# Masked decays of a gated DeltaNet mixer: products moved from GpSimd to ScalarE, masks into a TensorE pass, more buffers for the q, k, v sums

## Chip, cores and metric

The kernel runs on one core of a Trainium2 chip. The metric is the device time of one execution, in microseconds (us). Before the change it was 1235.73 us, the median of three runs (1235.57 to 1237.52).

## What is computed

A two-layer encoder on 256 tokens of width 1024. Each layer is half a feed-forward block, a mixer, and half a feed-forward block again. The change touches the mixer alone. One projection of the normed input, `h @ w_in`, gives the q, k, v of a gated DeltaNet (4 heads of 128), its output gate z, its decay logits, the two latents of an attention branch (8 heads) and two merge gates. The parts of the reference that the change bears on:

```python
def centred_short_conv(x, w):      # 5 taps over the sequence, then SiLU
    y = lax.conv_general_dilated(x, w[:, None, :], (1,), [(2, 2)], ...)
    return jax.nn.silu(y)
...
g = -exp(A_log) * softplus(a + dt_bias)                    # log decay per token and head, <= 0
gc = cumsum(to_chunks(g), axis=-1)
incl = jnp.tril(jnp.ones((C, C), bool))
decay = exp(where(incl, gc[..., :, None] - gc[..., None, :], -inf))
lower = where(strict, einsum("bhik,bhjk->bhij", kb, kc) * decay, 0.0)
unit = eye(C) + lower
uw = triangular_solve(unit, rhs, lower=True, unit_diagonal=True)
```

The recurrence runs in both directions over the sequence, each with its own decays, and the results are summed, normed, gated and projected; the attention branch is added, and the sum is projected back to the residual.

## The kernel before

Tokens lie in two tiles of 128. Every large product takes three passes on TensorE: a value is split in a rounded part and a rest (`whi` and `wlo` for weights, `xh` and `xl` or a pair `fr` for activations), and the passes are whi by xh, wlo by xh, whi by xl (L148 to L150, L557). For each tile of weights a DMA brings `raw`, ScalarE rounds it (L130, `whi`) and VectorE subtracts (L131, `wlo`). A `wlo` or a `whi` that comes late stops TensorE, and both engines take their instructions in a fixed order.

The order of the mixer's first half, as the code calls it: `rstd_row`, `qkv_group(2)`, the projection for beta, decay logits and the q latent, `qkv_group(3)`, `qkv_group(0)`, the projection for the kv latent, `gdn_scalars`, `gdn_decay(0)`, `lengths(4)`, `latent(cq)`, `qkv_group(1)`, `gdn_decay(1)`, `latent(ckv)`, `gdn_coeffs`, `gdn_la(1)`, `gdn_la(0)`, `mla_dense(0)`, `mla_heads`, `gdn_base`, then the projection for z. A scheduler merges these calls into one fixed order for each engine, by priority; `tc.high_priority(offset=n)` moves what stands under it forward by n places, as far as its inputs allow.

`qkv_group(grp)` makes two blocks of 128 channels of q (groups 0, 1), k (2, 3) or v (4, 5). Its 48 matmuls sum in a PSUM tile `acc`; VectorE scales the sum by the row `rb` into `pre` (L565), which is 4 columns wider than the sequence, with zeros at the rim (L563, L564, on GpSimd); ten VectorE instructions per group (L571 twice, L573 eight times) make the five taps into `cv`; ScalarE takes the tanh (L577, `th`) and VectorE finishes (L578) into `qkT`. `pre`, `cv` and `th` have one buffer each, and `lengths` uses the one of `cv` as well, for the squares of q or k (L586, on GpSimd). So the scaling of a group waits until the taps of the group before it are done, and its PSUM tile stays taken until then.

`gdn_decay(t)` makes, for token tile t and both directions d, the 128 by 128 decays of 4 heads at once. The log decays are split in `gh` and `gl`. For each of the two GpSimd multiplies an inclusive triangular mask (`m_le` or `m_ge`) by the log decay of each token, all heads in one instruction of 512 columns (L743, tile `pr`, three buffers); TensorE multiplies by the strict mask of the other side (L744), which sums the log decays between two tokens; ScalarE takes the exponential (L746, `g`); GpSimd multiplies by the inclusive mask again, to clear what lies on the wrong side (L755). `gdn_la` multiplies k by q and k (L763) and VectorE joins that with the decays (L767, `LA`). `gdn_base` starts the inversion of the triangular matrices: transposes on VectorE (L791, L796), 30 short GpSimd instructions in a chain (L805, L807), then blocks on TensorE (L839 and on).

Of the kernel before, what the change touches and what calls it, by code (L numbers as in the profile page):

```python
# [11 lines left out]
F32 = mybir.dt.float32  # L12
# [25 lines left out]
def encoder_trunk(ctx: ExitStack, tc: tile.TileContext, x, positions, norm_ffn1, ffn1_w_gate, ffn1_w_up,  # L38
# [286 lines left out]
    def mixer_consts(tmp):  # L325
# [30 lines left out]
        m_le = tri(const.tile([P, P], F32, name="m_le"), ALU.is_ge, -1, 1)  # L356
        m_ge = tri(const.tile([P, P], F32, name="m_ge"), ALU.is_ge, 1, -1)
        mr_gt, mr_lt = (const.tile([P, P], F32R, name=n) for n in ("mr_gt", "mr_lt"))
        V.tensor_copy(out=mr_gt, in_=tri(tp[:, 192:192 + P], ALU.is_gt, 1, -1))
        V.tensor_copy(out=mr_lt, in_=tri(tp[:, 320:320 + P], ALU.is_gt, -1, 1))  # L360
# [47 lines left out]
        for mul in (2.0 ** 11, 1.0):  # L408
# [4 lines left out]
            for c in split_const(per, 4):  # L413
# [7 lines left out]
        mc.update(alog=alog, dtb=dtb, ones=ones, m_le=m_le, m_ge=m_ge, mr_gt=mr_gt, mr_lt=mr_lt, half=half, mlo=mlo, mup=mup,  # L421
                  eye16=eye16, cos_t=cos_t, sin_t=sin_t)


    def mixer(l, next_gain):
# [4 lines left out]
        alog, dtb, ones, m_le, m_ge, mr_gt, mr_lt, half, mlo, mup, eye16, cos_t, sin_t = (  # L430
            mc[n] for n in ("alog", "dtb", "ones", "m_le", "m_ge", "mr_gt", "mr_lt", "half", "mlo", "mup", "eye16", "cos_t",
                            "sin_t"))
        with tc.tile_pool(name="mix", bufs=1) as mp:
            def t2(tag, bufs, shape=(P, NH, P)):
# [85 lines left out]
            def gdn_scalars():  # L520
                A.activation(out=beta, in_=ba[:, :, 0:8], func=AF.Exp, scale=-1.0)
                V.tensor_scalar(out=beta, in0=beta, scalar1=1.0, scalar2=None, op0=ALU.add)
                V.reciprocal(out=beta, in_=beta)
                V.tensor_tensor(out=sa, in0=ba[:, :, 8:16], in1=dtb[:, l:l + 1, :].to_broadcast([P, NT, 8]), op=ALU.add)

                V.scalar_tensor_tensor(out=se, in0=sa, scalar=-1.0, in1=sa, op0=ALU.mult, op1=ALU.min)
                A.activation(out=se, in_=se, func=AF.Exp)
                V.tensor_scalar(out=su, in0=se, scalar1=1.0, scalar2=None, op0=ALU.add)
                V.tensor_scalar(out=sc_, in0=su, scalar1=-1.0, scalar2=None, op0=ALU.add)
                V.tensor_tensor(out=sc_, in0=se, in1=sc_, op=ALU.subtract)  # L530
                A.activation(out=glog, in_=su, func=AF.Ln)
# [14 lines left out]
            def qkv_group(grp):  # L546
# [34 lines left out]
            def lengths(c0):  # L581

                pss = gdp()[:, :4 * NT * 32].rearrange("p (c t s) -> p c t s", c=4, t=NT)
                for c in (0, 2):
                    sq = t2("cv", 1, (P, 2, S))
# [143 lines left out]
                    V.tensor_tensor(out=nV[t], in0=ev4(pv), in1=bc(nk_[:, t, :]), op=ALU.mult)  # L729

            Es = {}
            gsp = [mp.tile([P, NT, 8], F32R, name=n) for n in ("gh", "gl")]

            def gdn_decay(t):

                for d in range(2):
                    lo_m, hi_m = (mr_gt, m_le) if d == 0 else (mr_lt, m_ge)
                    g4 = glog[:, t, d * 4:d * 4 + 4]
                    hb = hi_m[:, None, :].to_broadcast([P, NH, P])
                    pe = gdp()  # L740
                    for i in range(2):
                        gm = t2("pr", 3).bitcast(F32R)
                        G.tensor_tensor(out=gm, in0=hb, in1=bc(gsp[i][:, t, d * 4:d * 4 + 4].bitcast(F32)), op=ALU.mult)  # L743
                        T.matmul(pe, lhsT=lo_m, rhs=gm.rearrange("p h d -> p (h d)"), start=(i == 0), stop=(i == 1))  # L744
                    E = g2()
                    A.activation(out=E, in_=ev4(pe), func=AF.Exp)  # L746
                    if t == d:

                        V.tensor_copy(out=cs[d], in_=E[:, :, P - 1 if d == 0 else 0])
                    else:  # L750
                        pg = gdp()
                        T.matmul(pg[:, :NH], lhsT=hi_m, rhs=g4, start=True, stop=True)
# [366 lines left out]
```

## Time and profile before

| what | value |
|---|---|
| three runs, us | 1235.57, 1237.52, 1235.73 |
| profiled execution, us | 1238.92 |
| its span, us | 1237.2 |
| mean granted TensorE clock | 0.985 of full |
| TensorE busy | 1204.2 us, 97% |
| VectorE busy | 770.9 us, 62% |
| ScalarE busy | 622.4 us, 50% |
| GpSimd busy | 132.3 us, 11% |
| mixer of layer 0 | about 190 to 422 us |
| mixer of layer 1 | about 798 to 1042 us |

Times inside the trace are microseconds from the start of the span; a column that gives the mean of one instruction is in nanoseconds. The granted clock is a share of TensorE's full speed. The profiled execution is 3.2 us above the median, and its span leaves 1.7 us outside.

### The profile page before, as it was taken

How to read it: one execution, taken by the hardware profiler on the slowest of the kernel's cores; microseconds unless marked ns; L12 is line 12 of the kernel's file. 1: busy time of each engine (PE TensorE's matmuls, PEld its weight loads, DVE VectorE, ACT ScalarE, POOL GpSimd, SP SyncE). 2: the span in 40 equal slices, each digit the busy share in tenths (PEclk: the TensorE clock that was granted, in tenths of full speed). 3: DMA queues.
4: the chain of work that ended last, by engine and by line, in shares of the span. 5: the costliest groups of instructions: out<-in, count | busy, mean ns of one | idle time of the engine just before them, and what ended most of it. 6: DMA issues, size and time to landing. Idle time of an engine off the chain costs nothing.

```text
span 1237.2 us, 17605 instructions
## 1 busy us (share of the span) xinstructions
PE 1204.2 (97%) x7064; PEld 1016.9 (82%) x7064; DVE 770.9 (62%) x1125; ACT 622.4 (50%) x911; POOL 132.3 (11%) x238
## 2 busy tenths in 40 slices
PE   9999999899999999999999999997999999999997
PEld 6888889778778888888888888897778888888886
DVE  5665556986857665554555554588858676555554
ACT  6554445547455454444454453465455455544443
POOL 1000001454101000000000000015540000000010
PEclk9999999989899999999999999998998999999999
DMA  7564555445222555556555556553453135565552
GB/s 265 181 197 144 201 188 179 139 125 174 94 88 103 171 185 189 176 173 207 187 178 187 186 170 194 182 158 122 124 168 104 69 138 186 178 198 180 191 187 85
DMA packets 114576, 202.70 MB, mean 164 GB/s; under 512 B 4107, under 2 KB 30399, under 8 KB 114495
## 3 DMA queue, kind: packets, MB, share of 16 engines
q1 hardware_dynamic: 114031, 200.52, 49.9%
q8 instruction: 55, 0.90, 0.3%
q10 hardware_dynamic: 464, 1.06, 0.2%
q14 instruction: 26, 0.21, 0.1%
HBM read 200.52 MB, written 1.05 MB: 163 GB/s over the span
## 4 chain that ended last, share of the span: by engine, by line
PE 87%; DVE 5%; POOL 4%; ACT 2%; issue 2%; DMA 0%; POOLq 0%; SPq 0%; ACTq 0%
PE acc L148 24%; PE acc L149 24%; PE acc L150 24%; PE acc L557 4%; PE ms L198 2%; DVE wlo L131 2%; POOL t L807 1%; PE ms L665 1%; POOL bt L805 1%; PE gd L148 1%; PE gd L149 1%; PE gd L150 1%; PE gd L938 1%; DVE cv L573 1%; PE gd L763 1%
## 5 line engine op out<-in xcount | busy, mean ns | idle before, releaser
L131 DVE TENSOR_TENSOR wlo<-raw,whi 128x1024 fp32r<-128x1024 f32 (+3 forms) x388 | 470.4, 1215 | 368.4 <-ACT whi L130 365.9
L130 ACT CAST whi<-raw 128x1024 fp32r<-128x1024 f32 (+3 forms) x388 | 399.3, 1033 | 424.0 <-PE acc L150 384.1
L149 PE MATMUL acc<-wlo,xh 128*128 128x512 f32 (+3 forms) x968 | 360.6, 374 | 0.0
L150 PE MATMUL acc<-whi,xl 128*128 128x512 f32 (+3 forms) x968 | 357.4, 372 | 0.0
L148 PE MATMUL acc<-whi,xh 128*128 128x512 f32 (+3 forms) x968 | 344.8, 376 | 0.1
L149 PEld LDWEIGHTS acc<-wlo,xh 128*128 128x128 f32 x968 | 182.4, 188 | 29.5 <-issue 0.4
L148 PEld LDWEIGHTS acc<-whi,xh 128*128 128x128 f32 x968 | 181.5, 189 | 30.3 <-ACT xh L115 0.8
L150 PEld LDWEIGHTS acc<-whi,xl 128*128 128x128 f32 x968 | 182.1, 188 | 29.3
L149 PE MATMUL acc<-wlo,hh 128*128 128x512 f32 x352 | 137.4, 390 | 0.0
L150 PE MATMUL acc<-whi,hl 128*128 128x512 f32 x352 | 137.1, 390 | 0.0
L148 PE MATMUL acc<-whi,hh 128*128 128x512 f32 x352 | 127.3, 392 | 0.0
L150 PEld LDWEIGHTS acc<-whi,hl 128*128 128x128 f32 x352 | 66.1, 188 | 13.8
L148 PEld LDWEIGHTS acc<-whi,hh 128*128 128x128 f32 x352 | 66.1, 188 | 13.7
L149 PEld LDWEIGHTS acc<-wlo,hh 128*128 128x128 f32 x352 | 66.1, 188 | 13.3
L148 PE MATMUL acc<-whi,fr 128*128 128x512 f32 (+1 forms) x152 | 60.3, 403 | 9.1 <-DVE pre L565 7.9
L149 PE MATMUL acc<-wlo,fr 128*128 128x512 f32 (+1 forms) x152 | 59.9, 396 | 0.0
L150 PE MATMUL acc<-whi,fr 128*128 128x512 f32 (+1 forms) x152 | 57.5, 395 | 2.4 <-DVE fr L116 2.4
L557 PE MATMUL acc<-xl,whi 128*128 128x256 f32 x192 | 55.3, 288 | 0.0
L557 PE MATMUL acc<-xh,wlo 128*128 128x256 f32 x192 | 54.2, 292 | 1.0 <-DVE wlo L131 1.0
L557 PE MATMUL acc<-xh,whi 128*128 128x256 f32 x192 | 54.9, 289 | 0.0
L573 DVE SCALAR_TENSOR_TENSOR cv<-pre,ccol,cv 128x256 f32<-128x256 f32 x96 | 51.5, 569 | 0.1
L563 POOL MEMSET pre<- 128x4 f32 x12 | 1.2, 104 | 425.3 <-PE acc L150 341.0
(298 smaller groups left out, 1271.9 us busy)
## 6 DMA issues: line engine op xcount, KB each, us to landing
raw<-in_ffn_w_up_dram SPq DMA_DIRECT2D x40, 1024.0 KB, 5.1
raw<-in_ffn_w_down_dram SPq DMA_DIRECT2D x40, 1024.0 KB, 4.9
raw<-in_ffn_w_gate_dram SPq DMA_DIRECT2D x38, 1024.0 KB, 5.0
raw<-in_w_in_dram SPq DMA_DIRECT2D x32, 1024.0 KB, 5.0
raw<-in_w_out_dram SPq DMA_DIRECT2D x8, 1024.0 KB, 4.9
raw<-in_ffn_w_gate_dram SPq DMA_DIRECT2D x12, 512.0 KB, 3.7
raw<-in_ffn_w_up_dram SPq DMA_DIRECT2D x8, 512.0 KB, 3.7
raw<-in_ffn_w_down_dram SPq DMA_DIRECT2D x8, 512.0 KB, 3.3
```

The costliest lines, as they stand in the source:

```text
L130: A.copy(out=hi[:, :n * w], in_=raw[:, k0 * w:(k0 + n) * w])
L131: V.tensor_tensor(out=lo[:, :n * w], in0=raw[:, k0 * w:(k0 + n) * w], in1=hi[:, :n * w].bitcast(F32), op=ALU.subtract)
L148: T.matmul(ps[t][:, :n], lhsT=a1, rhs=w[0], start=start, stop=False)
L149: T.matmul(ps[t][:, :n], lhsT=a1, rhs=w[1], start=False, stop=False)
L150: T.matmul(ps[t][:, :n], lhsT=a2, rhs=w[0], start=False, stop=stop)
L198: T.transpose(out=pt[:, i * S + t * P:i * S + (t + 1) * P], in_=srcs[t][:, (j + i) * P:(j + i + 1) * P], identity=ident)
L557: T.matmul(pc[:, c].rearrange("p (t s) -> p t s", s=P), lhsT=w[:, cc], rhs=a, start=(i == 0), stop=(i == len(terms) - 1))
L573: V.scalar_tensor_tensor(out=cv[:, c], in0=pre[:, c, d:d + S], scalar=wc, in1=cv[:, c], op0=ALU.mult, op1=ALU.add)
L665: T.matmul(sc[:, t * S:(t + 1) * S], lhsT=qT[:, t * P:(t + 1) * P], rhs=kT, start=True, stop=True)
L763: T.matmul(pa[:, (h - hp) * 256:(h - hp + 1) * 256], lhsT=qkT[:, 4 + h, t * P:(t + 1) * P], rhs=qkT[:, h:h + 5:4, t * P:(t + 1) * P], star ...
L805: G.tensor_tensor(out=tv, in0=M[:, b + 1:16, b:b + 1].to_broadcast([P, na, nb]), in1=Y[:, b:b + 1, 0:nb].to_broadcast([P, na, nb]), op=ALU ...
L807: G.tensor_tensor(out=Y[:, b + 1:16, 0:nb], in0=Y[:, b + 1:16, 0:nb], in1=tv, op=ALU.add)
```

## The change

Masks `m_le` and `m_ge` stay, and the strict masks become negated copies `n_gt`, `n_lt`. The product of a mask by the log decays is taken on ScalarE, head by head: four ACTIVATE instructions of 128 columns with the log decay as scale (after, L747) in place of one GpSimd product of 512. The log decays are scaled by -2^-14 as they are split. A third TensorE pass (after, L751) adds a large whole number where the mask is to clear, and the exponential multiplies by 2^14, so that what is to be cleared gets a large negative exponent. The GpSimd product after the exponential (L755) goes.

For groups 0 to 3 the scaled sums lie in the ring `gate`, which has 6 buffers and stood unused here; `cv` has two buffers; the tanh is written over the scaled sums. The padding goes: the middle tap (all 256 columns) comes first and the others cover 254 or 255 columns. The scaling of the sums (after, L566) has high priority by 150 places. `gdn_decay(0)` moves behind `qkv_group(1)` and `gdn_decay(1)`.

```diff
-                pre = t2("pre", 1, (P, 2, S + 4))
-                cv = t2("cv", 1, (P, 2, S))
-                G.memset(pre[:, :, 0:2], 0.0)
-                G.memset(pre[:, :, S + 2:S + 4], 0.0)
-                V.tensor_tensor(out=pre[:, :, 2:S + 2], in0=pc, in1=rb[...], op=ALU.mult)
+                pre = t2("gate", 6, (P, 2, S)) if grp < 4 else t2("pre", 1, (P, 2, S))
+                cv = t2("cv", 2, (P, 2, S))
+                with tc.high_priority(offset=150):
+                    V.tensor_tensor(out=pre, in0=pc, in1=rb[...], op=ALU.mult)
...
-                th = t2("th", 1, (P, 2, S))
+                th = pre
...
-                        G.tensor_tensor(out=gm, in0=hb, in1=bc(gsp[i][...]), op=ALU.mult)
-                        T.matmul(pe, lhsT=lo_m, rhs=gm..., start=(i == 0), stop=(i == 1))
+                        with tc.high_priority(offset=0):
+                            for h in range(NH):
+                                A.activation(out=gm[:, h, :], in_=hi_m.bitcast(F32), func=AF.Copy,
+                                             scale=gsp[i][:, t, d * 4 + h:d * 4 + h + 1].bitcast(F32))
+                        T.matmul(pe, lhsT=lo_m, rhs=gm..., start=(i == 0), stop=False)
+                    T.matmul(ev4(pe), lhsT=hi_m, rhs=lo_m[:, None, :]..., start=False, stop=True)
-                    A.activation(out=E, in_=ev4(pe), func=AF.Exp)
+                    A.activation(out=E, in_=ev4(pe), func=AF.Exp, scale=1.0 / GS)
-                    G.tensor_tensor(out=E, in0=E, in1=hb, op=ALU.mult)
...
-            gdn_decay(0)
             lengths(4)
             cqT = latent(cq, QL, 0, G_Q + 3 * l)
             qkv_group(1)
             gdn_decay(1)
+            gdn_decay(0)
```

On VectorE, around the scaling of group 0's sums in layer 0 (L565 before, L566 after; `acc` is the PSUM tile), before:

```order
L573 SCALAR_TENSOR_TENSOR cv<-pre,ccol,cv 128x256
L131 TENSOR_TENSOR wlo<-raw,whi 128x288
L573 SCALAR_TENSOR_TENSOR cv<-pre,ccol,cv 128x256
L536 TENSOR_TENSOR glog<-glog,alog 128x16
L131 TENSOR_TENSOR wlo<-raw,whi 128x1024
L565 TENSOR_TENSOR pre<-acc,rb 128x2x256
L578 SCALAR_TENSOR_TENSOR qkT<-th,cv 128x512
L113 TENSOR_TENSOR gl<-glog,gh 128x16
```

and after:

```order
L535 TENSOR_TENSOR glog<-glog,sc 128x16
L566 TENSOR_TENSOR gate<-acc,rb 128x512
L575 SCALAR_TENSOR_TENSOR cv<-gate,ccol,cv 128x255
L131 TENSOR_TENSOR wlo<-raw,whi 128x864
L575 SCALAR_TENSOR_TENSOR cv<-gate,ccol,cv 128x255
L536 SCALAR_TENSOR_TENSOR glog<-sa,glog 128x16
L572 TENSOR_SCALAR cv<-gate,ccol 128x256 x2
L575 SCALAR_TENSOR_TENSOR cv<-gate,ccol,cv 128x254
L131 TENSOR_TENSOR wlo<-raw,whi 128x288
```

Group 0's sums are scaled while the last taps of group 3 are still to come, instead of behind them all.

On VectorE, around the scaling of group 1's sums, some 20 rows on, before:

```order
L573 SCALAR_TENSOR_TENSOR cv<-pre,ccol,cv 128x256
L131 TENSOR_TENSOR wlo<-raw,whi 128x768
L573 SCALAR_TENSOR_TENSOR cv<-pre,ccol,cv 128x256 x2
L131 TENSOR_TENSOR wlo<-raw,whi 128x384
L565 TENSOR_TENSOR pre<-acc,rb 128x2x256
L578 SCALAR_TENSOR_TENSOR qkT<-th,cv 128x512
L630 TENSOR_SCALAR mv<-acc,lrs 128x256 x2
L131 TENSOR_TENSOR wlo<-raw,whi 128x1024 x3
L571 TENSOR_SCALAR cv<-pre,ccol 128x256 x2
```

and after:

```order
L575 SCALAR_TENSOR_TENSOR cv<-gate,ccol,cv 128x254
L566 TENSOR_TENSOR gate<-acc,rb 128x512
L131 TENSOR_TENSOR wlo<-raw,whi 128x768
L116 SCALAR_TENSOR_TENSOR fr_2265<-ms,gcol,fr_2264 128x256
L580 SCALAR_TENSOR_TENSOR qkT<-gate,cv 128x512
L131 TENSOR_TENSOR wlo<-raw,whi 128x384
L572 TENSOR_SCALAR cv<-gate,ccol 128x256 x2
L575 SCALAR_TENSOR_TENSOR cv<-gate,ccol,cv 128x254 x2
```

Group 1's scaling moved ahead of two weight subtractions, and its taps follow without the weight subtractions of the next projection between.

On ScalarE, at the decays (`g` is a decay tile; `pr` there is the scaled mask for L747, the kv latent for L475 and L510, after L476 and L511), before:

```order
L112 CAST gh<-glog 128x16
L130 CAST whi<-raw 128x1024
L475 ACTIVATE pr<-acc,rstd 128x256 x2
L130 CAST whi<-raw 128x1024
L510 ACTIVATE junk,lss<-pr 128x256 x2
L115 ACTIVATE fr_2250<-ms,gcol 128x256
L746 ACTIVATE g_2087<-gd 128x512
```

and after:

```order
L115 ACTIVATE gh<-glog 128x16
L130 CAST whi<-raw 128x1024
L476 ACTIVATE pr<-acc,rstd 128x256
L747 ACTIVATE pr<-m_le,gh 128x128 x4
L476 ACTIVATE pr<-acc,rstd 128x256
L130 CAST whi<-raw 128x1024
L511 ACTIVATE junk,lss<-pr 128x256
L747 ACTIVATE pr<-m_le,gl 128x128 x4
L115 ACTIVATE fr_2264<-ms,gcol 128x256
L511 ACTIVATE junk,lss<-pr 128x256
L747 ACTIVATE pr<-m_ge,gh 128x128 x4
L130 CAST whi<-raw 128x768
```

Fours of L747 now stand between the eviction of the kv latent's two halves, and ahead of weight casts.

## Rows read from the trace of the kernel before

**Rows 1.** The page, part 1: busy time, share of the span, instructions

```profile
PE 1204.2 (97%) x7064; PEld 1016.9 (82%) x7064; DVE 770.9 (62%) x1125; ACT 622.4 (50%) x911; POOL 132.3 (11%) x238
```

**Rows 2.** Waits of TensorE: engine, line, waited for: us, times, longest

```profile
PE acc L148 <- DVE pre L565: 7.9, 2, 3.9
...
PE ms L651 <- ACT qk L654: 2.8, 2, 1.4
PE acc L150 <- DVE fr L116: 2.4, 2, 1.2
PE gd L744 <- POOL pr L743: 2.2, 2, 1.1
```

**Rows 3.** Windows: stretch, us, PE, PEld, DVE, ACT, POOL busy, clock, DMA, GB/s

```profile
230.00:270.00 40.00, 33.75 (x187) 28.22 (x185) 34.08 (x52) 17.45 (x34) 29.73 (x33) 0.91 0.43 141
841.00:881.00 40.00, 33.76 (x187) 28.21 (x185) 34.09 (x52) 17.46 (x34) 29.72 (x33) 0.91 0.44 140
...
246.00:250.00 4.00, 2.13 (x7) 2.16 (x8) 4.00 (x8) 2.30 (x4) 1.18 (x3) 0.50 0.40 131
...
314.00:318.00 4.00, 1.77 (x59) 1.48 (x62) 3.04 (x7) 1.86 (x5) 0.00 (x0) 0.89 0.00 0
318.00:322.00 4.00, 3.42 (x39) 2.94 (x31) 3.72 (x8) 2.36 (x5) 0.00 (x0) 0.50 0.05 11
```

**Rows 4.** Timeline of VectorE: start, length, instruction, count, idle before

```profile
208.27 1.27 DVE L573 SCALAR_TENSOR_TENSOR cv<-pre,ccol,cv 128x256 f32<-128x256 f32 x3
209.46 1.22 DVE L131 TENSOR_TENSOR wlo<-raw,whi 128x1024 fp32r<-128x1024 f32 x1
...
239.16 0.47 DVE L116 SCALAR_TENSOR_TENSOR fr<-ms,gcol,fr 128x256 fp32r<-128x256 f32 x1
...
239.62 3.13 DVE L573 SCALAR_TENSOR_TENSOR cv<-pre,ccol,cv 128x256 f32<-128x256 f32 x3
...
247.04 0.68 DVE L565 TENSOR_TENSOR pre<-acc,rb 128x512 f32<-128x512 f32 x1
```

**Rows 5.** Timeline of TensorE, same columns

```profile
247.87 0.66 PE L148 MATMUL acc<-whi,fr 128*128 128x384 f32 x1 [3.94 <-DVE pre L565]
248.32 0.52 PE L149 MATMUL acc<-wlo,fr 128*128 128x384 f32 x1
...
252.16 0.39 PE L149 MATMUL acc<-wlo,fr 128*128 128x384 f32 x1
...
272.42 1.78 PE L763 MATMUL gd<-qkT 128*128 128x256 f32 x4 [0.21 <-DVE qkT L578]
273.99 1.91 PE L665 MATMUL ms<-qk 96*128 96x256 f32 x4
...
278.19 0.33 PE L148 MATMUL acc<-whi,fr 128*128 128x384 f32 x1
...
280.28 0.34 PE L148 MATMUL acc<-whi,fr 128*128 128x384 f32 x1
280.45 1.02 PE L763 MATMUL gd<-qkT 128*128 128x256 f32 x4
...
317.29 1.07 PE L839 MATMUL gd<-XC,LA 32*32 32x32 f32 x64 [1.71 <-DVE XC L816]
```

**Rows 6.** Instructions of GpSimd by line: count, ns least/middle/most, first and last start

```profile
L743 POOL TENSOR_TENSOR pr<-m_le,gh x4: 1451/1734/2019, 230.9 to 847.5; 128x512 fp32r<-128x512 f32 x4
...
L755 POOL TENSOR_TENSOR g<-g,m_le x4: 1298/1387/1478, 240.0 to 870.9; 128x512 f32<-128x512 f32 x4
```

**Rows 7.** Timeline of GpSimd, of the powers behind the lengths

```profile
265.07 2.98 POOL L598 TENSOR_TENSOR rqk<-ssq,neghalf 128x4 f32<-128x4 f32 x2
```

**Rows 8.** Instructions of ScalarE by line, columns as in Rows 6

```profile
L962 ACT ACTIVATE junk<-g x16: 309/310/312, 384.4 to 998.4; 128x128 bf16<-128x128 f32 x16
```

**Rows 9.** Timeline of ScalarE: two scaled evictions, and the tanh of group 1

```profile
231.67 0.83 ACT L475 ACTIVATE pr<-acc,rstd 128x256 f32<-128x256 f32 x2
...
269.84 0.63 ACT L577 ACTIVATE th<-cv 128x512 f32<-128x512 f32 x1 [4.93 <-DVE cv L573]
```

More of the change, by code (lines that the diff above doesn't have):

```diff
@@ L353, in tri @@
             return m
[L356 to L360, printed above, removed]
+        m_le, m_ge, n_gt, n_lt = (const.tile([P, P], F32R, name=n) for n in ("m_le", "m_ge", "n_gt", "n_lt"))
+        V.tensor_copy(out=m_le, in_=tri(tp[:, 192:192 + P], ALU.is_ge, -1, 1))
+        V.tensor_copy(out=m_ge, in_=tri(tp[:, 320:320 + P], ALU.is_ge, 1, -1))
+        for m, cm, c0 in ((n_gt, 1, 192), (n_lt, -1, 320)):
+            V.tensor_scalar(out=m, in0=tri(tp[:, c0:c0 + P], ALU.is_gt, cm, -cm), scalar1=-1.0, scalar2=None, op0=ALU.mult)
         half = const.tile([P, 2], F32, name="half")
@@ L420, in mixer_consts @@
         V.tensor_scalar(out=cos_t, in0=cos_t, scalar1=-2.0, scalar2=1.0, op0=ALU.mult, op1=ALU.add)
-        mc.update(alog=alog, dtb=dtb, ones=ones, m_le=m_le, m_ge=m_ge, mr_gt=mr_gt, mr_lt=mr_lt, half=half, mlo=mlo, mup=mup,
+        mc.update(alog=alog, dtb=dtb, ones=ones, m_le=m_le, m_ge=m_ge, n_gt=n_gt, n_lt=n_lt, half=half, mlo=mlo, mup=mup,
                   eye16=eye16, cos_t=cos_t, sin_t=sin_t)
@@ L429, in mixer @@
         wl_ = w_in[l]
-        alog, dtb, ones, m_le, m_ge, mr_gt, mr_lt, half, mlo, mup, eye16, cos_t, sin_t = (
-            mc[n] for n in ("alog", "dtb", "ones", "m_le", "m_ge", "mr_gt", "mr_lt", "half", "mlo", "mup", "eye16", "cos_t",
+        alog, dtb, ones, m_le, m_ge, n_gt, n_lt, half, mlo, mup, eye16, cos_t, sin_t = (
+            mc[n] for n in ("alog", "dtb", "ones", "m_le", "m_ge", "n_gt", "n_lt", "half", "mlo", "mup", "eye16", "cos_t",
                             "sin_t"))
@@ L560, in qkv_group @@
                     vT[grp - 4] = ysb[0][:, (grp - 4) * 512:(grp - 3) * 512].rearrange("p (c s) -> p c s", s=S)
-                pre = t2("pre", 1, (P, 2, S + 4))
-                cv = t2("cv", 1, (P, 2, S))
-                G.memset(pre[:, :, 0:2], 0.0)
-                G.memset(pre[:, :, S + 2:S + 4], 0.0)
-                V.tensor_tensor(out=pre[:, :, 2:S + 2], in0=pc, in1=rb[:, None, :].to_broadcast([P, 2, S]), op=ALU.mult)
+                pre = t2("gate", 6, (P, 2, S)) if grp < 4 else t2("pre", 1, (P, 2, S))
+                cv = t2("cv", 2, (P, 2, S))
+                with tc.high_priority(offset=150):
+                    V.tensor_tensor(out=pre, in0=pc, in1=rb[:, None, :].to_broadcast([P, 2, S]), op=ALU.mult)
                 for c in range(2):
                     ch = grp * 2 + c
-                    for d in range(5):
+                    for d in (2, 0, 1, 3, 4):
                         wc = ccol[:, l * 60 + d * 12 + ch:l * 60 + d * 12 + ch + 1]
-                        if d == 0:
-                            V.tensor_scalar(out=cv[:, c], in0=pre[:, c, 0:S], scalar1=wc, scalar2=None, op0=ALU.mult)
-                        else:
-                            V.scalar_tensor_tensor(out=cv[:, c], in0=pre[:, c, d:d + S], scalar=wc, in1=cv[:, c],
+                        if d == 2:
+                            V.tensor_scalar(out=cv[:, c], in0=pre[:, c], scalar1=wc, scalar2=None, op0=ALU.mult)
+                        else:
+                            o, i = (slice(2 - d, S), slice(0, S + d - 2)) if d < 2 else (slice(0, S + 2 - d), slice(d - 2, S))
+                            V.scalar_tensor_tensor(out=cv[:, c, o], in0=pre[:, c, i], scalar=wc, in1=cv[:, c, o],
                                                    op0=ALU.mult, op1=ALU.add)
-                th = t2("th", 1, (P, 2, S))
+                th = pre
                 A.activation(out=th, in_=cv, func=AF.Tanh, scale=0.5)
@@ L731, in mixer @@
             Es = {}
+            GS = 2.0 ** -14
             gsp = [mp.tile([P, NT, 8], F32R, name=n) for n in ("gh", "gl")]
@@ L736, in gdn_decay @@
                 for d in range(2):
-                    lo_m, hi_m = (mr_gt, m_le) if d == 0 else (mr_lt, m_ge)
+                    lo_m, hi_m = (n_gt, m_le) if d == 0 else (n_lt, m_ge)
                     g4 = glog[:, t, d * 4:d * 4 + 4]
-                    hb = hi_m[:, None, :].to_broadcast([P, NH, P])
                     pe = gdp()
@@ L742, in gdn_decay @@
                         gm = t2("pr", 3).bitcast(F32R)
-                        G.tensor_tensor(out=gm, in0=hb, in1=bc(gsp[i][:, t, d * 4:d * 4 + 4].bitcast(F32)), op=ALU.mult)
-                        T.matmul(pe, lhsT=lo_m, rhs=gm.rearrange("p h d -> p (h d)"), start=(i == 0), stop=(i == 1))
+                        with tc.high_priority(offset=0):
+                            for h in range(NH):
+                                A.activation(out=gm[:, h, :], in_=hi_m.bitcast(F32), func=AF.Copy,
+                                             scale=gsp[i][:, t, d * 4 + h:d * 4 + h + 1].bitcast(F32))
+                        T.matmul(pe, lhsT=lo_m, rhs=gm.rearrange("p h d -> p (h d)"), start=(i == 0), stop=False)
+                    T.matmul(ev4(pe), lhsT=hi_m, rhs=lo_m[:, None, :].to_broadcast([P, NH, P]), start=False, stop=True)
                     E = g2()
-                    A.activation(out=E, in_=ev4(pe), func=AF.Exp)
+                    A.activation(out=E, in_=ev4(pe), func=AF.Exp, scale=1.0 / GS)
                     if t == d:
@@ L751, in gdn_decay @@
                         pg = gdp()
-                        T.matmul(pg[:, :NH], lhsT=hi_m, rhs=g4, start=True, stop=True)
+                        T.matmul(pg[:, :NH], lhsT=hi_m.bitcast(F32), rhs=g4, start=True, stop=True)
                         A.activation(out=egc[d], in_=pg[:, :NH], func=AF.Exp)
-                    G.tensor_tensor(out=E, in0=E, in1=hb, op=ALU.mult)
                     Es[d, t] = E
```

4 lines of the change are left out of this document (2 added, 2 removed).

## The prediction

> **What bounds the kernel now.** I read the busy shares first. TensorE is busy for 1204.2 us of 1237.2 [rows 1], so about 33 us is all its idle time, and no other engine comes near: the kernel ends when TensorE has done its work, and a change pays where it takes away a wait of TensorE, a pass of TensorE, or a stretch at low clock. Then I read the waits of TensorE by what ended them [rows 2]. The largest one is at L148, the first product behind the q, k, v groups: 7.9 us in two waits, one per layer, 3.9 each, ended by L565 on VectorE, the scaling of group 1's sums. Two others lie in the same stretch: 1.2 us per layer for VectorE's part of a latent (L116) and 1.1 for a GpSimd product (L743). One more, 1.4 per layer, is for L654, a copy on ScalarE. All come twice, once in each mixer, and the two windows of 40 us that hold them agree within 0.01 us of busy time on each engine [rows 3]; so I work for one layer and double.
>
> In that window VectorE is busy for 34.1 us of 40, GpSimd for 29.7, ScalarE for 17.5, at a granted clock of 0.91 [rows 3]. VectorE is late because its own work is stretched: three taps of the convolution take 1.27 us at 208 us, where GpSimd is idle, and 3.13 us at 239.62, where GpSimd runs its products; the L116 beside them, which reads PSUM, takes 0.47 [rows 4]. So the L565 that TensorE waits for comes at 247.04 [rows 4], and TensorE goes on at 247.87 [rows 5].
>
> A wait here has a second price. [...] From 247.87 to 252.16 it issues 13 matmuls of 384 columns in 4.29 us; from 278.19 to 280.28, at full clock, 12 of them take 2.09, or 0.174 each [rows 5]. 13 at 0.174 are 2.26, so 2.03 us are lost. The same shows at 272.42 and 273.99: two fours of 256 columns take 1.78 and 1.91 us, where a four takes 1.02 at 280.45 [rows 5]; that is 0.76 and 0.89, together 1.65.
>
> **The change part by part, per layer.**
>
> *The wait for L565 goes.* In the new order the scaling of group 0 stands amid the taps of group 3, and from there to the scaling of group 1 VectorE has 12 taps, one pair of first taps, three full weight subtractions and two short ones, and some ten small instructions. A tap is 0.42 or less when GpSimd is quiet (three in 1.27), a full weight subtraction 1.22 with some overlap [rows 4]. That sums to about 12.4 us: 12 by 0.40, 3 by 1.13, 1.3 for the short weights, 0.6 each for one scaling, the pair and the finish of group 3, the rest for small ones. It begins at about 225 by the trace before, so group 1 is scaled at about 238.5, which is when its matmuls are done, instead of 247.04. The wait of 3.94 goes whole [rows 5], with it the half clock behind it, 2.03. The 1.2 for L116 [rows 2] goes by the same cause, since the taps ahead of it are no longer stretched. Gain 3.94 + 2.03 + 1.2 = 7.17. The small memsets of the padding leave GpSimd too; nothing waits for them, and I count nothing.
>
> *The wait for L654 goes.* On ScalarE that copy stands behind the tanh of group 1, which waits 4.93 us for its taps until 269.84 [rows 9]. In the new order these taps follow their scaling at once and don't wait for the squares' buffer. Gain 1.4 [rows 2], the 0.21 at 272.42 [rows 5] and the half clock of 1.65: 3.26.
>
> *GpSimd's products.* Eight L743 and four L755, of 1.1 to 2.0 us and 1.3 to 1.5 us [rows 6], some 18 us per layer, leave an engine that TensorE waited for once, 1.1 us [rows 2]. In its place comes a wait for ScalarE: the eviction of the kv latent's second half now stands behind four of the new ACTIVATEs, and TensorE's transposes of it wait. The nearest row for one is an ACTIVATE of 128 columns, 0.31 us [rows 8]; an eviction that also takes a scale from a column, but of 256 columns, is 0.42 in a pair [rows 9]. I take 0.31, the same width: four are 1.24. Net -0.14.
>
> *The new ACTIVATEs.* 32 per layer by 0.31 are 9.9 us (13.3 by 0.42). ScalarE is busy for 17.5 of 40 us in the window [rows 3], and with them for 27.4 of what will be some 31; I cost them at nothing beyond the 1.24 above, since ScalarE waits there for TensorE and VectorE most of the time. If that cover is gone they delay weight casts, which stand behind them; that is the third rival.
>
> A full 512 columns on ScalarE take 0.63 us (the tanh, [rows 9]), so one head at a time costs 1.24 where one wide instruction would cost half. [...]
>
> *The third TensorE pass.* Four per layer of 512 columns. At 0.174 for 384 [rows 5] that is 0.232 each, 0.93 per layer (1.9 if all fell into half clock). They lie on TensorE, which is the bound, so it counts whole.
>
> *Other new waits.* With TensorE some 9 us earlier, what is late next? On VectorE the weights of the z projection stand behind the copy of the rotary key into the attention's k. That copy waits for the rotary products on GpSimd, which now stand behind the powers of the lengths, a pair of 2.98 us [rows 7]. I take half of that, 1.5, with 0 and 2.98 as ends. The second product of the first decay waits for four ACTIVATEs that start behind a latent's square: 0.3, with 0 and 1.24 as ends. Together 1.8.
>
> *The inversion.* From 314 to 322 TensorE is idle for 2.81 us (4 less 1.77, 4 less 3.42), and its clock is 0.50 in the second half [rows 3]. The first L839 waits there for a chain that begins with the last L763 at 280.45 and runs through VectorE, 30 GpSimd steps and VectorE again to 317.29 [rows 5]. The change touches none of these steps and shifts their start with TensorE's. I take this gap as it is; the first two rivals say how else it may go.
>
> **The sum.** 7.17 + 3.26 - 0.14 - 0.93 - 1.8 = 7.56 us per layer, 15.1 for two. The profiled execution took 1238.9, 1.7 above its span and 3.2 above the median of the runs; taken from the median of 1235.7, the forecast is 1220.6. By its unknown costs alone: with no new wait at all (1.8 and 1.24 back) it is 10.6 per layer, 1214.5; with the ends against it (1.5 more at the z weights, 0.9 more at the decays, 0.4 for slower ACTIVATEs, no half clock regained at 272) 3.0 per layer, 1229.7. It is likely within 1215 to 1227.
>
> **The rivals.**
>
> *The inversion's gap closes too.* If the chain gets ahead of TensorE by as much as VectorE is relieved (29.7 us of GpSimd's 40 in the window fall to a third, and the taps that now lie between the LA steps are done earlier), the 2.81 us go and the half clock on 3.42 us of busy time, 1.71: 4.5 more per layer, 1211.6. Against it: the chain's start is one of TensorE's own instructions.
>
> *The inversion's gap widens.* The new orders put about 2 us less of TensorE's work between the last L763 and the first L839 (about 32 us by the durations of the trace, against 34 to 34.6 before). If the chain holds its 36.8 us, the idle time there grows by 2 us, and a longer stand makes another stretch at half clock of about 1.7: 3.7 per layer are given back, 1228.
>
> *ScalarE becomes the bound (the slower side).* It has 9.9 us more in a stretch that is to shrink by about 9, in a fixed order with weight casts behind every four. Each us of that which reaches TensorE takes one from the gain; at 7.6 per layer exposed the change is level, and with all 9.9 exposed it is 2.3 per layer slower, 1240.4. For it: two of the waits that I count already stand on ScalarE. Against it: ScalarE is idle for 22.5 of the 40 us [rows 3].
>
> *The waits only move.* The scaling is early, but the next late thing, such as the tanh of group 1 or the weights behind it, holds TensorE as long as before, and the third pass adds 1.9: the gain of 15 shrinks to nothing, about 1235. For it: VectorE is the fullest engine after TensorE in the window, 34.1 of 40, and gains no time but what contention took.
>
> **How the numbers follow.** Forecast 0.50; inversion closes 0.14; inversion widens 0.20; waits only move 0.07; ScalarE the bound 0.09. 0.2% is about 2.5 us, what a measurement of this kernel can tell from no change. The first three are faster: 0.84; the fourth is within: 0.07; the fifth slower: 0.09. The range takes in the forecast's bounds and both rivals of the inversion, 1211 to 1231, which leaves out the last two cases (0.16) and little else.
>
> **What the profile of the changed kernel would show.** Right: no wait of TensorE at L148 for the scaling; the clock at full in the 20 us around it; three taps in about 1.25 us throughout; GpSimd below a third of the window; a wait near 1.2 us at the transposes of the kv latent, ended by ScalarE; no wait at L651; L839 waiting about 1.7 us still. Wrong: waits of TensorE for `whi` (ScalarE) in that stretch, taps that stay stretched, ACTIVATEs of 0.4 us or more, or an L839 wait that grows to 4 us.

## The result and the profile after

The changed kernel takes 1219.69 us, the median of four runs (1218.56 to 1221.2), against 1236.62 for the kernel before in the same comparisons. The ratio is 0.9858, with a 95% interval of 0.9839 to 0.9878: 1.4% faster. The forecast was 1220.6 in a range of 1211 to 1231. The profiled execution took 1220.7 with a span of 1219.0, so 18.2 us less span than before; the medians differ by 16.9.

Part 1 of the page of the changed kernel, to be held against [rows 1]:

```profile
PE 1195.3 (98%) x7072; PEld 1010.0 (83%) x7072; DVE 757.6 (62%) x1127; ACT 639.8 (52%) x975; POOL 102.6 (8%) x190
```

TensorE is busy for 8.9 us less although it has eight passes more: that is clock regained, as the windows below show (0.96 in both mixers before, 0.99 and 1.00 after). ScalarE has 64 instructions and 17.4 us more, GpSimd 48 instructions and 29.7 us less. The waits of TensorE in the changed kernel, to be held against [rows 2] (line, what ended the wait, us, times, longest):

```profile
PE acc L149 <- DVE wlo L131: 4.1, 4, 1.5
PE gd L844 <- DVE XC L821: 3.3, 2, 1.7
PE ms L494 <- ACT pr L476: 2.1, 2, 1.1
...
PE acc L148 <- ACT whi L130: 0.9, 2, 0.4
```

The four waits of [rows 2] are gone, and four come in their place, per layer: 1.53 and 0.53 us for weights from VectorE, 1.06 for the kv latent, 0.44 for a weight cast on ScalarE. The stretch of 40 us that answers to the first row of [rows 3], and the mixers of both layers whole, from the first transposes behind their norm to those of the next block (columns as in [rows 3]):

```profile
225.00:265.00 40.00, 37.41 (x233) 32.44 (x232) 34.91 (x72) 32.49 (x74) 13.45 (x17) 1.00 0.49 162
...
199.80:423.20 223.40, 216.69 (x1700) 186.41 (x1699) 169.40 (x330) 135.23 (x259) 42.23 (x68) 0.99 0.42 137
801.90:1024.00 222.10, 215.09 (x1700) 184.78 (x1699) 169.25 (x330) 135.00 (x259) 42.22 (x68) 1.00 0.43 138
```

And of the kernel before, the same two mixers (the table ahead of the prediction gives their bounds more roughly, some 10 us early in layer 0):

```profile
198.90:431.20 232.30, 220.32 (x1696) 189.39 (x1695) 176.12 (x330) 126.42 (x227) 57.43 (x90) 0.96 0.41 132
809.90:1042.20 232.30, 220.36 (x1697) 189.39 (x1696) 176.21 (x330) 126.50 (x227) 57.36 (x90) 0.96 0.41 131
```

A mixer is 8.9 us shorter in layer 0 and 10.2 in layer 1. Length less busy time is the idle time of TensorE: 12.0 us before, 6.7 and 7.0 after. The rest of the gain is busy time, 3.6 and 5.3 us less, although the third pass adds 0.9.

On VectorE of the changed kernel most taps run at their quiet pace, and the scaling of group 1 (L566) waits for TensorE and not the other way round (start, length, instruction, idle before):

```profile
234.12 1.25 DVE L575 SCALAR_TENSOR_TENSOR cv<-gate,ccol,cv 128x255 f32<-128x255 f32 x1
...
237.15 0.86 DVE L575 SCALAR_TENSOR_TENSOR cv<-gate,ccol,cv 128x255 f32<-128x255 f32 x2
...
239.81 0.69 DVE L566 TENSOR_TENSOR gate<-acc,rb 128x512 f32<-128x512 f32 x1 [0.49 <-PE acc L558]
...
252.07 2.88 DVE L131 TENSOR_TENSOR wlo<-raw,whi 128x1024 fp32r<-128x1024 f32 x2
```

Two taps in 0.86 us, where three took 3.13 in [rows 4]; the scaling is at 239.81 where it was at 247.04. Some of what still meets GpSimd is still stretched: one tap beside the squares of the lengths takes 1.25 us, and two weight subtractions beside the rotary products 2.88, where one takes 1.22 when GpSimd is quiet [rows 4]. Not all of it is: a weight subtraction at 232.98, beside the same squares, takes 1.21.

### The profile page after: what moved, and what is told of

Its sections match the earlier page's. It is cut to its first block, busy times and chain, and to the rows that moved or that the text cites. A ratio compares the mean times of both kernels' runs of the same rounds, so it can differ in the third digit from the quotient of the medians.

```text
span 1219.0 us, 17632 instructions
## 1 busy us (share of the span) xinstructions
PE 1195.3 (98%) x7072; PEld 1010.0 (83%) x7072; DVE 757.6 (62%) x1127; ACT 639.8 (52%) x975; POOL 102.6 (8%) x190
## 3 DMA queue, kind: packets, MB, share of 16 engines
q10 hardware_dynamic: 464, 1.06, 0.2%
## 4 chain that ended last, share of the span: by engine, by line
PE 85%; DVE 7%; ACT 3%; POOL 3%; issue 2%; DMA 1%; SPq 0%; POOLq 0%; ACTq 0%
PE acc L150 23%; PE acc L149 23%; PE acc L148 23%; PE acc L558 4%; DVE wlo L131 2%; PE ms L198 2%; ACT whi L130 1%; POOL bt L810 1%; POOL t L812 1%; DVE cv L575 1%; PE gd L148 1%; PE gd L149 1%; PE gd L150 1%; PE ms L667 1%; PE gd L961 1%
## 5 line engine op out<-in xcount | busy, mean ns | idle before, releaser
L150 PEld LDWEIGHTS acc<-whi,xl 128*128 128x128 f32 x968 | 182.4, 189 | 29.7
L262 ACT ACTIVATE sil<-acc,rstd 128x512 f32<-128x512 f32 (+1 forms) x48 | 31.0, 654 | 29.5 <-PE acc L150 29.5
L558 PEld LDWEIGHTS acc<-xh,whi 128*128 128x128 f32 x192 | 37.2, 195 | 0.6 <-issue 0.4
```

Of the source, the lines that this page charges most:

```text
L150: T.matmul(ps[t][:, :n], lhsT=a2, rhs=w[0], start=False, stop=stop)
L262: A.activation(out=sil[t][:, :w], in_=ps, func=AF.Silu, scale=rstds[0][:, t:t + 1])
L558: T.matmul(pc[:, c].rearrange("p (t s) -> p t s", s=P), lhsT=w[:, cc], rhs=a, start=(i == 0), stop=(i == len(terms) - 1))
```

## The experiments

All kernels are timed against the kernel before (ratio with its interval). In the comparisons "the change" is the 1219.7 above. The scheduler merges the calls anew for every variant, so each variant may differ from its neighbour in more places than the diff names; two runs below show what that can do. No run leaves out the `tc.high_priority(offset=150)` of the diff, so what it is worth is not shown.

**The parts alone.** Which half of the change carries the gain, the places for the sums or the decays?

```diff
# e1_buffers_only: the changed kernel with gdn_decay, its masks, split and call order as before
-    A.activation(out=gm[:, h, :], ..., scale=gsp[i][...])
+    G.tensor_tensor(out=gm, in0=hb, in1=bc(gsp[i][...]), op=ALU.mult)
-    T.matmul(ev4(pe), lhsT=hi_m, rhs=lo_m..., start=False, stop=True)
+    G.tensor_tensor(out=E, in0=E, in1=hb, op=ALU.mult)
# e2_masks_only: the changed kernel with pre, cv, th in one buffer each and padded, as before
```

> The places alone: the ring gate for the scaled sums, two buffers of cv, the tanh in place, no padding; masks and products stay on GpSimd as before, decays in the old order. Theory 1 (the wait for the scaling was a matter of buffers): the scaling of group 1 comes at about 243 instead of 247, since group 0 is scaled early, though taps stay stretched while GpSimd runs (three in about 3 us); TensorE's wait of 3.9 us at L148 falls to below 1, and the one of 1.4 us behind the tanh of group 1 goes: some 6 us per layer, 1224. Theory 2 (it was the stretching of VectorE by GpSimd): the wait stays at 2.5 us or more with its half clock, and the time is 1230 or above.

> The decays alone: masked on ScalarE and by the third TensorE pass, in the new order; pre, cv and th with one buffer each as before. Theory 1 (buffers): group 1's sums still wait for the taps of group 0, TensorE waits 2 us or more at L148 and falls to half clock: 1230 or above. Theory 2 (stretching): VectorE gets back the 6 us that the stretched instructions cost between 231 and 248, the scaling of group 1 comes at about 241, TensorE waits less than 0.5 us for it: 1223 to 1226. If both alone give over 10 us, they remove the same wait and the sum of the two is above what the whole change gives (17).

e1 measured 1229.78 us, ratio 0.994 (0.9925 to 0.9955); e2 1226.51, ratio 0.9913 (0.9898 to 0.9928). So the places alone give 7.3 us, the decays alone 10.6, and together 17: nearly a sum. I had thought that both remove the same wait, and so that each alone would get most of the gain. The wait does go both times, but more hangs on VectorE than that. In e1 the scaling does come early (243.70) and the wait for it is gone, as theory 1 has it, but the time is 6 us above its 1224: beside a busy GpSimd VectorE gets through 57 instructions in 39.17 us, and TensorE waits for other work of VectorE and what hangs on it. The window of e1, and then TensorE's longest waits in the whole execution:

```profile
225.00:265.00 40.00, 35.44 (x218) 29.83 (x217) 39.17 (x57) 21.78 (x39) 30.92 (x29) 1.00 0.43 131
```

```profile
PE acc L148 <- ACT whi L130: 4.6, 2, 2.3
PE acc L150 <- DVE fr L116: 4.0, 4, 1.7
PE acc L149 <- DVE wlo L131: 3.1, 6, 0.8
```

The longest, 2.31 us in layer 0, is for a weight cast on ScalarE, which stands behind copies that wait for VectorE's `LA` (ScalarE, then TensorE):

```profile
274.53 2.60 ACT L794 COPY g<-LA 32x256 f32<-32x256 f32 x4 [3.99 <-DVE LA L768]
...
278.61 0.50 PE L148 MATMUL acc<-whi,xh 128*128 128x512 f32 x1 [2.31 <-ACT whi L130]
```

In e2 no wait for the scaling is left either, with the old places: GpSimd is busy for 1.45 us of the 12 from 230, where it was for 10.16 before, and the scaling comes when it does in the changed kernel (239.81):

```profile
239.80 0.68 DVE L567 TENSOR_TENSOR pre<-acc,rb 128x512 f32<-128x512 f32 x1
```

That is theory 2, with a time 0.5 us above its range. What is left there is a wait of 1.82 us for the latent on ScalarE and one of 1.98 for the inversion, per layer.

**The order of the calls, and the first products.**

```diff
# e4_decay_order: the changed kernel
+            gdn_decay(0)
             lengths(4)
             ...
             gdn_decay(1)
-            gdn_decay(0)
# e5_gpsimd_products: the changed kernel, third TensorE pass kept
-    for h in range(NH): A.activation(out=gm[:, h, :], ..., func=AF.Copy, scale=...)
+    G.tensor_tensor(out=gm, in0=hi_m..., in1=bc(gsp[i][...]), op=ALU.mult)
# e10_products_old_order: both edits
```

> The changed kernel with gdn_decay(0) called before lengths(4), as before the change. If the order of the calls carries a part of the gain, ScalarE's 16 first ACTIVATEs crowd the casts of weights ahead of group 1 and the time rises by 2 to 4 us per layer (1224 to 1228); if it is a matter of ScalarE's spare time alone, within 1.5 us of 1219.7.

> The changed kernel with the first products (mask by log decay) back on GpSimd, eight of 512 columns per layer, and the third TensorE pass kept (no product after the exponential). Theory 1: places matter, GpSimd's products little: within 3 us of 1219.7, and the wait of 1.06 us for the kv latent's second half goes with the ACTIVATEs. Theory 2: taps stretch again (three in 2 to 3 us) and the time rises by 4 us or more, 1224 to 1230. ScalarE's busy time falls by about 10 us per layer.

> The e5 kernel (first products on GpSimd, mask by the third TensorE pass) with gdn_decay(0) called before lengths(4) as before the change. It differs from e1 only in the mask behind the exponential: e1 has it on GpSimd (four products of 512 per layer), this one in a TensorE pass. If the 10 us between e1 (1229.8) and e5 (1219.7) come from that mask leaving GpSimd, this is 1220 to 1222; if they come from the order of the decays, it is 1228 or above.

e4 measured 1220.14 (ratio 0.9864, 0.9847 to 0.988), e5 1219.74 (0.9862, 0.9847 to 0.9877), e10 1217.97 (0.9844, 0.9826 to 0.9862). None can be told from the change. Moving `gdn_decay(0)` is worth nothing that can be measured, and neither is moving the eight first products to ScalarE, once the sums have their places and the mask is a TensorE pass. e10 has the lowest median of all kernels, but its interval overlaps that of the change, so it isn't shown to beat it.

With these products on GpSimd the taps are stretched again, two in 1.65 us, and the scaling comes 3.9 us later than in the changed kernel, yet TensorE has no wait for it. On VectorE of e10, and its window:

```profile
240.00 1.65 DVE L575 SCALAR_TENSOR_TENSOR cv<-gate,ccol,cv 128x254 f32<-128x254 f32 x2
...
243.68 0.67 DVE L566 TENSOR_TENSOR gate<-acc,rb 128x512 f32<-128x512 f32 x1
```

```profile
225.00:265.00 40.00, 37.52 (x231) 32.17 (x230) 39.39 (x73) 23.34 (x41) 24.80 (x25) 1.00 0.51 162
```

VectorE is as full as in e1, but gets through 73 instructions where e1 has 57: a full VectorE alone is not what costs e1 its time.

e10 and e1 differ only in the mask behind the exponential (and the scaling of the log decays that goes with it): four products per layer on GpSimd, or a TensorE pass. That is worth 11.8 us. The two traces show how: VectorE's rows agree within some hundredths until 245 us, then GpSimd of e1 takes its masks (L756), the squares and the rotary products stand behind them, and much of the VectorE work beside them is stretched: the weight subtraction of 384 columns that comes next takes 1.64 us where it takes 0.55 in e10, and the one of 1024 columns after it 2.31 where it takes 1.26. The end of group 1, on VectorE, in e1 and then in e10:

```profile
261.27 0.68 DVE L579 SCALAR_TENSOR_TENSOR qkT<-gate,cv 128x512 f32<-128x512 f32 x1
```

```profile
257.39 0.68 DVE L580 SCALAR_TENSOR_TENSOR qkT<-gate,cv 128x512 f32<-128x512 f32 x1
```

Behind it the first inversion product of layer 0 starts at 308.76 in e1 and at 302.48 in e10.

**That mask alone.** Would it have done without the places?

```diff
# e13_pe_mask_only: the kernel before with
-    T.matmul(pe, lhsT=lo_m, rhs=gm..., start=(i == 0), stop=(i == 1))
+    T.matmul(pe, lhsT=lo_m, rhs=gm..., start=(i == 0), stop=False)
+    T.matmul(ev4(pe), lhsT=hi_m, rhs=lo_m..., start=False, stop=True)
-    G.tensor_tensor(out=E, in0=E, in1=hb, op=ALU.mult)
```

> The kernel before with only the product behind the exponential (four per layer of 512 columns on GpSimd) taken away and the third TensorE pass in its place; first products on GpSimd, buffers and order as before. It completes the table of parts. If that product alone is what counted, it gives with the old places about what it gives with the new ones (11.8 us between e1 and e10): 1225. If the first products matter where the places are scarce (they stretch the taps between 231 and 244, ahead of the scaling that TensorE waits for), the wait at L148 stays at 2.5 us or more and the time is 1230 to 1233, 4 us or more above e2 (1226.5).

It measured 1246.2, ratio 1.0071 (1.0048 to 1.0093): slower than before, which neither case had. Up to the inversion it gains: TensorE still waits 2.48 us for the scaling, as the second case has it, yet the first inversion product starts at 308.13 instead of 317.29 [rows 5]. Most of the loss is some 85 us later, at the end of the mixer, where TensorE now comes to the transposes of the gated output and waits for VectorE, which it did not before (TensorE, columns as in [rows 5]):

```profile
394.03 0.33 PE L494 MATMUL ms<-ident,g 128*128 128x128 f32 x1 [4.04 <-DVE g L976]
394.55 0.36 PE L494 MATMUL ms<-ident,g 128*128 128x128 f32 x1 [0.20 <-DVE g L976]
395.54 1.54 PE L494 MATMUL ms<-ident,g 128*128 128x128 f32 x6 [0.62 <-DVE g L976]
```

and the window of 10 us around them:

```profile
390.00:400.00 10.00, 5.02 (x15) 3.60 (x16) 5.51 (x19) 4.16 (x17) 2.01 (x2) 0.74 0.10 37
```

In the order of the kernel before, 34 matmuls of 512 columns of other projections stand on TensorE between the last product that makes that output and its first transpose; in e13 none does, so the norm between them on ScalarE, VectorE and GpSimd lies open. So this run doesn't price the mask in the old places; that stays open. It shows that a change which gains where it is made can lose more elsewhere, in an order that the scheduler makes.

**ScalarE's cover.** The third rival of the prediction, pushed:

```diff
# e6_double_act: the changed kernel, each masking ACTIVATE issued twice
-    for h in range(NH):
+    for h in [h for h in range(NH) for _ in range(2)]:
```

> The changed kernel with each of the 32 ACTIVATEs of 128 columns per layer issued twice (same output), so ScalarE has another 32 x 0.30 = 9.5 us per layer where it is 32.5 busy of 40 us. If ScalarE still had the 7.5 us of cover that its idle time there seems to show, 2 to 4 us per layer reach TensorE, 1224 to 1228. If nothing hides what comes on top, the whole 9.5 reach it: 1239. If ScalarE's queue has slack elsewhere, under 1 us per layer: 1221.

It measured 1232.05, ratio 0.9967 (0.9957 to 0.9978), 12.4 us above the change: more than my middle case (1224 to 1228), less than the whole 19. A mixer is 6.8 us longer in layer 0 and 6.5 in layer 1 for 8.9 and 9.1 us more of ScalarE's busy time, so about three quarters reach TensorE. The window of e6, and then TensorE's longest waits in the whole execution:

```profile
225.00:265.00 40.00, 35.08 (x203) 29.16 (x202) 30.22 (x64) 37.48 (x98) 9.63 (x15) 0.96 0.35 110
```

```profile
PE gd L749 <- ACT pr L747: 3.9, 4, 1.0
PE acc L558 <- DVE wlo L131: 3.1, 2, 1.5
```

ScalarE is full, 37.48 of 40, and TensorE waits for the masked log decays themselves. The change itself has used up most of the cover: 32.49 of 40.

**The new waits, taken away.** The changed kernel waits 1.06 us for the kv latent and 1.53 for weights. Do these count?

```diff
# e7_rope_early: rotary key ahead of group 1, powers of the lengths in one instruction
-                if hf == 0:
-                    rope(kr, krope, 1, tmp)
             cqT = latent(cq, QL, 0, G_Q + 3 * l)
+            rope(kr, krope, 1, ...)
             qkv_group(1)
-                for t in range(NT):
-                    G.tensor_tensor(out=rqk[:, t, c0:c0 + 4], ..., op=ALU.pow)
+                G.tensor_tensor(out=rqk[:, :, c0:c0 + 4], ..., op=ALU.pow)
# e8_kv_first: the masking ACTIVATEs are issued behind the second eviction of the kv latent
# e9_both: both edits
```

> The changed kernel with the rotary products of the key moved ahead of group 1 (GpSimd stands idle there) and the two powers of the lengths in one instruction. If TensorE's wait of 1.53 us for weights of the next projection comes from the copy that waits for GpSimd, as the trace says, it goes or falls below 0.5, 1.2 us per layer: 1217. If the weights are late for ScalarE's casts, the wait stays and the time too: 1219.7.

> The changed kernel with both halves of the kv latent evicted ahead of the first four masking ACTIVATEs. The wait of 1.06 us at the transposes (L494) goes; if nothing later takes it up, 1.0 us per layer: 1217.6; if the inversion's chain or a late weight takes it up, no change.

> e7 and e8 together. If both waits are independent, the gains add: 2.3 us per layer, 1215; if TensorE only reaches the next late thing sooner, no better than the better one of the two, 1217.

e7 measured 1220.8 (ratio 0.9873, 0.9856 to 0.989), e8 1220.2 (0.9872, 0.9857 to 0.9887), e9 1219.78 (0.987, 0.9856 to 0.9885): no gain that can be measured. The waits themselves went as expected, so the trace named their causes rightly. In e7 a longer wait for the inversion took up more than half of what went; TensorE at the first inversion product, in the changed kernel and then in e7:

```profile
307.35 0.75 PE L844 MATMUL gd<-XC,LA 32*32 32x32 f32 x64 [1.67 <-DVE XC L821]
```

```profile
306.46 0.75 PE L842 MATMUL gd<-XC,LA 32*32 32x32 f32 x64 [2.73 <-DVE XC L819]
```

TensorE is ready 1.95 us earlier and goes on 0.89 us earlier. In e8 half of the removed wait came back as two waits for VectorE ahead of that, of 0.25 and 0.23 us, and the inversion starts 0.12 us earlier.

**The inversion's wait, filled.** If that chain now holds TensorE, more work ahead of it should help:

```diff
# e11_v_groups_early: the changed kernel; e12_v_early_both: the same on e9
             dense(xh, xl, NKC, wl_, C_Z, 512, ev_z)
+            qkv_group(4)
+            qkv_group(5)
             inv_zero()
```

> The changed kernel with the two v groups called ahead of the inversion, so that by the order about 7 us more of TensorE's work lies between the last product of the LA step and the first of the inversion. If the inversion's chain (about 35 us in every run so far) is what now holds TensorE, the wait of 1.67 us for it goes and with it the half clock that follows in one layer of two: 2 to 3 us per layer, 1214 to 1216. If that wait only moves, to the steps of the inversion behind it, 1218 or above.

> e11 together with e9 (rotary key early, one power, kv latent evicted first). In e9 the removed waits came back as a longer wait for the inversion's chain (2.73 for 1.67 us). If the chain is what swallowed them, they count now: 1.5 to 2.5 us per layer below e11, 1210 to 1212. If not, the same as e11.

e11 measured 1227.02 (ratio 0.9918, 0.9901 to 0.9934), e12 1225.4 (0.9909, 0.9891 to 0.9927): slower than the change by 7.3 and 5.7 us, and e12 can't be told from e11. The wait at the inversion went, but a longer one came 5 us ahead of it. TensorE, and what VectorE does there, in e11:

```profile
311.31 0.81 PE L684 MATMUL ms<-ident,pr 128*128 128x128 f32 x4 [3.62 <-DVE pr L679]
```

```profile
308.10 2.18 DVE L815 TENSOR_SCALAR g<-t,half 128x256 f32<-128x256 f32 x2 [5.07 <-POOL t L812]
310.20 0.15 DVE L677 RECIPROCAL rs<-sm 128x2 f32<-128x2 f32 x1
...
310.94 0.57 DVE L679 TENSOR_SCALAR pr<-pr,rs 128x256 f32<-128x256 f32 x2
```

The instruction that waits for GpSimd's 30 steps stands in VectorE's queue ahead of the attention's normalisation, which TensorE needs. The chain still holds TensorE, only through VectorE's queue. That such work can be put into the gap with a gain isn't shown by these runs.

## Why the prediction was right, point by point

*The wait for the scaling* (7.17 us per layer with L116 and the half clock, 0.50 from 246 to 250 in [rows 3]): right. No wait of that kind is left, the clock is 1.00 over the 40 us, and the scaling came at 239.81 where I had 238.5; this execution runs 0.9 us late from the first loads on. e1 and e2 add that the early place and the quiet taps each remove the wait alone, so the step joined two causes of which either was enough. e5 and e10 add that quiet taps are not needed beside the early place: with the eight first products back on GpSimd there are other waits (2.5 us for `mv` in e5, 1.4 for L116 in e10), and the time is no longer. So the relief of GpSimd that counts beside the new places is the four masks (e10 against e1); the forecast priced all twelve products as one step. The taps take 0.43 us quiet (0.86 for two) and about 1.04 beside GpSimd's products (3.13 for three, [rows 4]).

*The wait for L654* (3.26): right. No wait at that product is left, and the clock, 0.85 from 270 to 274 and 0.73 from 274 to 278 in the kernel before, is 1.00 from 262 to 276 in the changed one.

*GpSimd's products* (net -0.14): in line with e5, where the eight of them back on GpSimd change no time that can be measured.

*The new ACTIVATEs.* Taken at 0.31 us each. They are issued 0.29 apart: four of them take from 232.94 to 234.11 until the next starts, though one alone lasts 0.38 to 0.42.

```profile
232.94 1.27 ACT L747 ACTIVATE pr<-m_le,gh 128x128 fp32r<-128x128 f32 x4
234.11 0.46 ACT L476 ACTIVATE pr<-acc,rstd 128x256 f32<-128x256 f32 x1
```

32 of them are 9.4 us. The wait that they cause, 1.24 in the sum, measured 1.06. I had costed the rest at nothing, and that held: in the window ScalarE went from 17.5 to 32.5 of 40 us, 81%, where I had reckoned with 27.4 of 31, 88%. I gave the rival of a bound on ScalarE 0.09; e6 shows that as much again would have lost three quarters of the gain, so there was less room than that number says.

*The other new waits* (1.8): the one for weights was taken at 1.5 and measured 1.53, in the place and by the chain that was named, as e7 shows by removing it. The 0.3 behind the second product didn't come; two of 0.44 and 0.53 at 277 to 279 us did, which I hadn't named; the first is for a cast on ScalarE, the third rival's kind of wait, in small.

*The inversion* (taken as unchanged): the wait is 1.67 where it was 1.71, but not for the reason given, that nothing changes there. From the last four L768 to the first inversion product it is 35.6 us instead of 36.8, and TensorE comes to its wait after 34.0 us instead of 35.1; both fell by about 1.2 us, which was luck. The start of that stretch in the changed kernel:

```profile
271.72 1.02 PE L768 MATMUL gd<-qkT 128*128 128x256 f32 x4
```

Two smaller waits beside it, 0.52 and 0.58 us before, are gone in layer 0. And the clock behind it is better. In windows of 2 us of the changed kernel, layer 0 and then layer 1:

```profile
306.00:308.00 2.00, 0.65 (x64) 0.64 (x64) 2.00 (x5) 1.33 (x3) 0.00 (x0) 1.00 0.00 0
308.00:310.00 2.00, 2.00 (x21) 1.97 (x10) 0.82 (x3) 1.18 (x6) 0.00 (x0) 0.55 0.00 0
310.00:312.00 2.00, 2.00 (x12) 2.00 (x12) 1.58 (x4) 1.74 (x3) 0.00 (x0) 0.60 0.03 8
...
908.00:910.00 2.00, 0.59 (x64) 0.59 (x64) 2.00 (x5) 1.39 (x3) 0.00 (x0) 1.00 0.00 0
910.00:912.00 2.00, 2.00 (x34) 1.96 (x21) 0.81 (x3) 1.12 (x5) 0.00 (x0) 1.00 0.00 0
```

In layer 0 it is 0.55 and 0.60 in two of these windows, in layer 1 it stays at 1.00. Before, it was 0.78 from 316 to 318 and still 0.51 from 322 to 324, so below full beyond the 322 us where [rows 3] end:

```profile
316.00:318.00 2.00, 0.71 (x52) 0.71 (x56) 1.04 (x4) 1.86 (x5) 0.00 (x0) 0.78 0.00 0
...
322.00:324.00 2.00, 2.00 (x9) 1.81 (x9) 2.00 (x5) 0.00 (x0) 0.00 (x0) 0.51 0.87 282
```

By TensorE's busy time and the missing share of the clock, window by window, that cost some 2.8 us before and costs 1.7 and nothing now, an estimate. That is the term that was mis-sized: the clock part of the first rival came true beside the forecast, wholly in one layer and in part in the other. The sum per layer was 7.56; it measured 8.9 and 10.2. Its idle part was 4.8 (7.85 of waits gone, 3.04 new) and measured 5.3 and 5.0; the clock was taken to give back 3.7 and gave 4.6 and 6.2 (3.6 and 5.3 less busy time, with the 0.93 of the third pass added); the 0.9 and 2.5 above the forecast are about what the inversion's clock gave. In the medians the whole came to 16.9 where I had 15.1.

*The second rival*, that the inversion's gap widens, is what the next steps met: in e7, e8 and e9 the chain or VectorE took back much of what was removed. It did not come true for this change, since the chain shrank along with TensorE's work.

*The signs.* All that were named as right were seen, but for two at the edge: one tap takes 1.25 us alone, and GpSimd is busy for 13.45 us of 40, a third and not less. One named as wrong was seen as well, ACTIVATEs of 0.4 us; it did no harm, since they are issued 0.29 apart.

What stays open: why the parts add up so closely. The runs show that each leaves waits that the other removes, but every variant has an order of its own, and e13 shows how much that alone can move.

## What to carry to other kernels

The wait for VectorE, busy for 34.1 of 40 us [rows 3], had two cures, an earlier place in its queue (e1) and a neighbour that slows it less (e2; two taps take 0.86 us in the changed kernel and 1.65 in e10); each removed the same wait, and yet the gains added, since each left waits behind that one which the other removed. A part of a change can also be worth nothing: eight products per layer moved to ScalarE gave no time that can be measured, four masks per layer moved to TensorE gave 11.8 us with the new places. When moving work to a spare engine, price it on that engine's busy share in the stretch after the change, not before: the stretch shrinks, and ScalarE went from 44% to 81% in it. Before taking away a small new wait, look for the next chain that ends at the same point: three variants here removed waits of 1 to 1.5 us and gained nothing that can be measured.

## What the runs showed of the hardware

The granted clock after the same wait wasn't the same. In the changed kernel TensorE waits 1.67 us at the inversion in layer 0 and 1.66 in layer 1, behind and ahead of the same instructions; the clock then falls to 0.55 in one and stays at 1.00 in the other. In e7 a wait of 2.73 us comes in both layers, and this time layer 0 keeps its clock and layer 1 loses it: its mixers are 221.4 and 224.0 us long. Behind that wait in e7, layer 0 and then layer 1:

```profile
308.00:310.00 2.00, 1.86 (x16) 1.69 (x15) 0.79 (x3) 2.00 (x6) 0.00 (x0) 1.00 0.00 0
...
908.00:910.00 2.00, 2.00 (x11) 2.00 (x11) 0.79 (x3) 2.00 (x6) 0.00 (x0) 0.50 0.00 0
```

So these waits came with a second price in one layer and without it in the other. The mixers of the two layers differ by 1.3 us in the changed kernel and 2.6 in e7, about the size of the differences between e4, e5, e7 to e10 and the change.

Joining the powers of the lengths saved nothing that shows: one instruction of 8 columns took 2.95 us in e7; the pair of 4 in its place took 2.52 (e1) to 3.29 us (the changed kernel), 2.98 before [rows 7]. The wait for weights went in e7 by the earlier rotary key, which was done at 238.9 us, ahead of the powers:

```profile
247.57 2.95 POOL L599 TENSOR_TENSOR rqk<-ssq,neghalf 128x8 f32<-128x8 f32 x1 [6.53 <-DVE ssq L596]
```

One and the same GpSimd product of 512 columns took 1.45 us at its quickest and 2.02 at its slowest [rows 6]. No run isolates what VectorE did beside it.
